# The per-layer gate of 704 tokens, computed as seven products per pair of output chunks

## The chip, the core and the metric

The kernel runs on one core of a Trainium2 chip. The core has a matmul engine (TensorE, PE in the profile), two engines for elementwise work (VectorE, DVE, and ScalarE, ACT), a slower one (GpSimd, POOL) and queues that start DMA transfers (here nearly all on SyncE, SP). The engines run side by side, each takes its own instructions in the order in which they stand in its queue, and semaphores tie them together. Matmuls write to PSUM, which has eight banks; everything else lies in SBUF. The metric is the device time of one execution in microseconds; the median of several runs counts.

## The reference

One layer of a decoder trunk is applied to 1056 tokens (1024 of a prompt, 32 of eight short continuations) with a width of 1024. What matters here is its last step, after mixing and feed-forward:

```
f = (silu(f @ w_gate) * (f @ w_up)) @ w_down
x = x + rms(f, n_ffn_post)
x = x + sigmoid(x @ w_ple_gate) * (p @ w_ple)
```

`x @ w_ple_gate` is the gate: a 1024 x 1024 product. `p @ w_ple` is the embedding product, from width 256 to 1024. The sum is the output `y`. Everything is float32; the kernel keeps that accuracy by splitting each operand into a high and a low part in a reduced format and adding three products (high x high, high x low, low x high).

## The kernel before

**Tiles.** Tokens lie along the free dimension, in three groups of 352: groups 0 and 1 (the 704 tokens of the title) and group 2. Channels lie on partitions, in 8 chunks of 128. One output tile is one chunk m of one group, 128 x 352. A full gate product for it takes 8 input chunks x 3 = 24 matmuls of 128 x 128 by 128 x 352; the embedding product takes 2 x 3 = 6.

**The stage.** Group 2 runs ahead of the others through the feed-forward part. At the end the order on TensorE is: the last down products of groups 0 and 1 (`last_down`), then `ple_out(0, m, 2)` for m = 1 to 7, then `ple_out(1, m, g)` for m = 7 down to 0 and g = 0, 1. `ple_out` (L1116) issues the embedding product (6 matmuls) and the gate product (24) into two PSUM banks; then ScalarE takes the sigmoid (L1126), VectorE multiplies (L1128) and adds x (L1130), and a DMA on SP writes the tile out (L1131).

**What comes ahead of it.** `ple_steps(g)` (L1062) is a generator, one for each group. It loads and splits the group's embedding input (`pl`, two DMAs, two casts, two subtractions), loads x from a scratch tensor, computes the norm, adds it to x for each half h of the channels (L1078, L1082: tiles `o` and `x2`), and splits the result with `f_operand` into operands (`fh`, `fl`) for TensorE, a cast on ScalarE (L164) and a subtraction on VectorE (L165), each 128 x 1408.

**The planner.** Between the products, `turn(n)` advances a clock counted in matmuls, and starts the next step of each pending generator (a chain) when it is due: each step names its load on VectorE, which is divided by a share (0.7 in this stage) and added up. `finish(...)` empties chains at once. So the planner sets where a step stands in the program. TensorE's order here is that of the program (`keep_in_program_order`); for the other engines the framework's scheduler takes the order of the program as a priority, and puts an instruction ahead of an earlier one when that one isn't ready by its reckoning.

**Weights.** A list ITEMS names the weights in the order of use. `need(k)` makes all items up to k + 4: a load of 512 KB into a raw buffer (tag `wr`, 3 buffers, `w_load`), then the split into high and low part (tag `wp`, 8 buffers of 4 KB per partition; `wh`, `wl`). A buffer comes free when its last reader is done. Activations lie in a pool of 27 buffers (tag `a`).

**Seven products.** The gate and up projections of the feed-forward part use a fast product for the tokens of groups 0 and 1 already: two output chunks (1, 2) and two token groups form a 2 x 2 block of products over the two channel halves, and seven half products replace eight. For it `t_sum` prepares four differences of operands (T1 to T4), and `w_sums` (L941) has GpSimd make four sums of weight halves in place in the raw buffers (L951, four operations of 128 x 512), which are then split like other weights (`sh`, `sl`). A quarter product is 4 x 3 = 12 matmuls (`ops4`). Before the change the per-layer gate does not use it.

Of the kernel before, what the change touches and what calls it, by code (L numbers as in the profile page):

```python
# [61 lines left out]
def trunk_kernel(  # L62
# [159 lines left out]
    for s, gs in WALK:  # L222
        pairs_of = []
        for i in range(SLAB):
# [9 lines left out]
            js = item("sums", jg, ju) if 0 in gs else None  # L234
# [16 lines left out]
    WPE[1] = [None] * 6 + WPE[0][6:]  # L251
    wp = WPE[0][-1][0]
    for m in reversed(range(6)):
        if m == 3:
            wp = direct_item(w_ple[0], [P, 2, 512])
        WPE[1][m] = wp, direct_item(w_pg[m], [P, KC, P])
# [3 lines left out]
    def need(k, ahead=LOOK):  # L260

        for i in range(len(made), min(k + ahead + 1, len(ITEMS))):
            kind, js = ITEMS[i]
            if kind == "direct":
                w_split(js[0])
                made[i] = pairs[js[0]]
            else:
                made[i] = w_sums(*(raws[ITEMS[j][1][0]] for j in js))
            for kind, js in ITEMS[i + 1 : i + 3]:
                if kind == "direct":  # L270
                    w_load(js[0])
        return made[k]
# [788 lines left out]

    def ple_steps(g):  # L1062

        pl = half(g, F32R, "pl")
        pls[g] = pl[:, 0:2, :], pl[:, 2:4, :]
        for k in range(2):
            pr = tmp(NS[g], "pr")
            nc.sync.dma_start(pr, p[:, k, OFF[g] : OFF[g + 1]])
            split(pl[:, k, :], pl[:, 2 + k, :], pr)
# [6 lines left out]
        for h in range(2):  # L1076
# [12 lines left out]
            x2s[g].append(f_operand(xh, g))  # L1089
            yield 10, 0  # L1090

# [24 lines left out]
    def ple_out(n, m, g):  # L1116
# [9 lines left out]
        se.activation(sg, pg[:, :N], AF.Sigmoid)  # L1126
# [5 lines left out]

    hid[:] = new_hid
    for m in range(FIRST):
        ple_out(0, m, 2)
# [6 lines left out]
    for m in range(FIRST, KC):  # L1142
        ple_out(0, m, 2)
# [93 lines left out]
```

## Time and profile before

| | |
|---|---|
| median of 3 runs | 1128.7 us (1128.33 to 1130.65) |
| profiled execution | 1130.04 us |
| its span | 1128.3 us |
| PE busy | 1116.1 us (99%) |
| DVE busy | 746.0 us (66%) |
| ACT busy | 440.4 us (39%) |
| POOL busy | 176.3 us (16%) |
| DMA, mean | 88 GB/s |

The span is the time from the first to the last recorded instruction; the execution's own time is a little longer. In rows of the profile, a line such as `L165 DVE TENSOR_TENSOR wl<-wr,wh` gives the line of the kernel, the engine, the operation and the tiles that it writes and reads, without their numbers. Times are in us from the start of the span; in square brackets stands how long the engine was idle before the instruction, and what ended that. L126 is the line of all matmuls, L164 and L165 are those of all splits, so tile names tell them apart: `wh` and `wl` are weights, `sh` and `sl` split sums, `fh` and `fl` operands, `o` the feed-forward output.

### The profile page before, as it was taken

What the parts mean: (1) busy time and instruction counts of PE and PEld (TensorE: products, weight loads), DVE (VectorE), ACT (ScalarE), POOL (GpSimd) and SP (SyncE); (2) the same over time, 40 slices, a digit from 0 to 9 for tenths busy, and PEclk for the clock granted to TensorE, in tenths of its full rate; (3) what the DMA queues carried; (4) which work ended last, traced back from release to release, by engine and by line L of the source; (5) the groups of instructions that cost most, each with busy time, mean ns of one, the idle gap of its engine ahead of it and who ended that gap; (6) DMA issues with size and microseconds to landing.
All of it is one profiled execution on the core that took longest, in us unless ns stands there. A gap on an engine that the chain in (4) does not pass through costs nothing.

```text
span 1128.3 us, 17581 instructions
## 1 busy us (share of the span) xinstructions
PE 1116.1 (99%) x7115; PEld 1093.3 (97%) x7115; DVE 746.0 (66%) x1238; ACT 440.4 (39%) x776; POOL 176.3 (16%) x149
## 2 busy tenths in 40 slices
PE   8999999999999999999999999999999999999998
PEld 8999987699999999999999999999999999999998
DVE  6667457876888965256555555557887877789532
ACT  7322266754555533331221313133424324366220
POOL 0045032200000032011111201111123123100000
PEclk9999999999999999999999999999999999999999
DMA  8121310172553312112110211112312222246211
GB/s 286 57 69 50 117 44 29 38 278 77 181 184 131 112 56 76 38 39 75 36 59 19 76 38 58 56 38 79 117 56 76 75 75 76 94 165 214 89 58 39
DMA packets 35265, 99.54 MB, mean 88 GB/s; under 512 B 4180, under 2 KB 14708, under 8 KB 35184
## 3 DMA queue, kind: packets, MB, share of 16 engines
q1 hardware_dynamic: 33856, 96.65, 25.3%
q10 hardware_dynamic: 1328, 1.77, 0.5%
q8 instruction: 56, 0.92, 0.3%
q14 instruction: 25, 0.20, 0.1%
HBM read 88.30 MB, written 10.11 MB: 87 GB/s over the span
## 4 chain that ended last, share of the span: by engine, by line
PE 91%; DVE 4%; ACT 2%; DMA 1%; issue 1%; POOL 1%; SPq 0%; POOLq 0%; ACTq 0%; DVEq 0%
PE b L126 90%; ACT a L625 1%; DMA xr<-in_x_dram 1%; DVE mx L617 1%; PE b L120 1%; POOL wr L951 0%; DVE a L662 0%; ACT wh L164 0%; DVE wl L165 0%; DVE h L364 0%; DMA c<-in_gains_dram 0%; DVE o L1078 0%; DVE x L1082 0%; POOL a L631 0%; DVE a L716 0%
## 5 line engine op out<-in xcount | busy, mean ns | idle before, releaser
L126 PE MATMUL b<-fh,wh 128*128 128x352 f32 x808 | 260.7, 323 | 0.0
L126 PE MATMUL b<-fh,wl 128*128 128x352 f32 x808 | 259.5, 321 | 0.0
L126 PE MATMUL b<-fl,wh 128*128 128x352 f32 x808 | 259.1, 321 | 0.0
L126 PE MATMUL b<-hid,wh 128*128 128x352 f32 x1056 | 253.0, 322 | 1.5 <-DVE o L1078 1.0
L164 ACT CAST wh<-wr 128x1024 fp32r<-128x1024 f32 (+1 forms) x139 | 142.9, 1030 | 262.7 <-PE b L126 226.8
L165 DVE TENSOR_TENSOR wl<-wr,wh 128x1024 fp32r<-128x1024 f32 (+1 forms) x139 | 170.7, 1231 | 61.9 <-ACT wh L164 61.7
L126 PEld LDWEIGHTS b<-hid,wh 128*128 128x128 f32 x1056 | 182.8, 188 | 2.4 <-PE b L126 1.3
L126 PE MATMUL b<-hid,wl 128*128 128x352 f32 x528 | 169.5, 321 | 0.0
L951 POOL TENSOR_TENSOR wr<-wr 128x512 f32<-128x512 f32 x44 | 63.5, 1442 | 628.1 <-DVE wl L165 452.5
L126 PEld LDWEIGHTS b<-fh,wl 128*128 128x128 f32 x808 | 152.0, 188 | 0.0
L126 PEld LDWEIGHTS b<-fl,wh 128*128 128x128 f32 x808 | 151.9, 188 | 0.0
L126 PEld LDWEIGHTS b<-fh,wh 128*128 128x128 f32 x808 | 151.6, 188 | 0.0
L1048 DVE TENSOR_TENSOR o<-o,b 128x352 f32<-128x352 f32 x240 | 115.0, 518 | 27.1 <-PE b L126 26.9
L126 PE MATMUL b<-fh,sh 128*128 128x352 f32 x352 | 113.6, 323 | 0.0
L126 PE MATMUL b<-fh,sl 128*128 128x352 f32 x352 | 113.2, 321 | 0.0
L126 PE MATMUL b<-fl,sh 128*128 128x352 f32 x352 | 112.9, 321 | 0.0
L126 PE MATMUL b<-h,wh 128*128 128x352 f32 x480 | 105.5, 326 | 1.0 <-ACT h L362 1.0
L165 DVE TENSOR_TENSOR sl<-wr,sh 128x1024 fp32r<-128x1024 f32 x44 | 53.8, 1223 | 75.4 <-ACT sh L164 75.4
L126 PEld LDWEIGHTS b<-hid,wl 128*128 128x128 f32 x528 | 99.3, 188 | 0.0
L164 ACT CAST sh<-wr 128x1024 fp32r<-128x1024 f32 x44 | 45.7, 1047 | 131.6 <-POOL wr L951 88.4
L126 PEld LDWEIGHTS b<-h,wh 128*128 128x128 f32 x480 | 82.5, 190 | 1.6 <-ACT h L362 1.3
L126 PEld LDWEIGHTS b<-fh,sl 128*128 128x128 f32 x352 | 66.3, 188 | 0.0
(152 smaller groups left out, 1597.8 us busy)
## 6 DMA issues: line engine op xcount, KB each, us to landing
wr<-in_w_gu_dram SPq DMA_DIRECT2D x64, 512.0 KB, 3.3
wr<-in_w_dn_dram SPq DMA_DIRECT2D x32, 512.0 KB, 3.3
wr<-in_w_pg_dram SPq DMA_DIRECT2D x14, 512.0 KB, 3.6
x<-in_x_dram SPq DMA_DIRECT2D x6, 704.0 KB, 10.9
x1d<-x SPq DMA_DIRECT2D x6, 704.0 KB, 3.6
x<-x1d SPq DMA_DIRECT2D x6, 704.0 KB, 6.4
out_y_dram<-yo SPq DMA_DIRECT2D x24, 176.0 KB, 1.9
wr<-in_w_out_b_dram SPq DMA_DIRECT2D x8, 512.0 KB, 3.9
```

Of the source, the lines that this page charges most:

```text
L120: ins = te.transpose(out, src, ident)
L126: ins = te.matmul(*args, **kw)
L164: fix(se.copy(hi, src))
L165: fix(ve.tensor_tensor(lo, src, hi.bitcast(F32), op=ALU.subtract))
L617: ve.tensor_reduce(mx, t, axis=AX.X, op=ALU.max)
L625: se.activation(t[:, c, :], t[:, c, :], AF.Exp, bias=nmx[:, c : c + 1], scale=scale, accum_out=sm[:, c : c + 1])
L951: ge.tensor_tensor(out, a, b, op=op)
L1048: ve.tensor_tensor(o, o, v, op=ALU.add)
```

## The change

For groups 0 and 1 the gate is computed as seven products per pair of chunks (1,0), (3,2), (5,4) and (7,6), as in the feed-forward part. Each pair has a first step (`ple_first`): two quarter products that give the tile of the odd chunk for group 0 directly, of which the first, P1, is kept. The first steps of all four pairs come ahead, for chunks 7, 5, 3 and 1. Then comes the rest of each pair (`ple_rest`), from (1,0) to (7,6): products with T4, T2, T3 and T1 and one with B22, and adds on VectorE, which give the other three tiles. In every tile the embedding product now stands behind the gate's (`ple_end`).

`ple_steps` no longer makes the operand B12, loads and splits the embedding input at its end, and for group 1 then makes T1, T2, T3 and T4 (`e_sum`), with each difference written over a tile of `o`. Of weights there are three new kinds: "home", the embedding weights, split into two buffers of the activation pool; "half", for which only the second half of the channels of the even chunk is split, into one buffer of `wp`; and "sums" on two raw weights. Only pair (1,0) finds its odd chunk's raw weight still there; the other pairs load it again. So the loads behind group 2's weights are: chunk 5, the embedding weights' first half, chunks 3, 1, 0, 3, 2, the embedding weights' second half, chunks 5, 4, 7, 6.

```diff
-    def w_split(j):
+    def w_split(j, home=None):
...
-        hi, lo = w_tile(shape, "wh"), w_tile(shape, "wl")
+        hi, lo = (home(shape, F32R) if home else w_tile(shape, s) for s in ("wh", "wl"))
...
+    PAIRS = ((1, 0), (3, 2), (5, 4), (7, 6))
+    W1 = {a: WPE[0][a] if a == KC - 1 else None for a, _ in PAIRS}
+    wp1 = WPE[0][-1][0]
+    wp0 = None
+    for a in (5, 3, 1):
+        if a == 3:
+            wp0 = item("home", add_plan(w_ple[0], [P, 2, 512]))
+        W1[a] = (wp0 if a < 4 else wp1), direct_item(w_pg[a], [P, KC, P])
+    W2 = {}
+    for a, b in PAIRS:
+        ja = ITEMS[W1[a][1]][1][0] if a == 1 else add_plan(w_pg[a], [P, KC, P])
+        jb = add_plan(w_pg[b], [P, KC, P])
+        if a == 5:
+            wp0 = item("home", add_plan(w_ple[1], [P, 2, 512]))
+        W2[a] = wp0, item("half", jb), item("sums", ja, jb)
...
-            if kind == "direct":
-                w_split(js[0])
+            if kind in ("direct", "home"):
+                w_split(js[0], act_tile if kind == "home" else None)
                 made[i] = pairs[js[0]]
+            elif kind == "half":
+                w_load(js[0])
+                t = w_tile([P, KC, P], "w2")
+                made[i] = t[:, 0:4, :], t[:, 4:8, :]
+                split(*made[i], raws[js[0]][:, 4:8, :])
             else:
-                made[i] = w_sums(*(raws[ITEMS[j][1][0]] for j in js))
+                for j in js:
+                    w_load(j)
+                made[i] = w_sums(*(raws[j] for j in js))
...
+    def e_sum(name):
+        (b11, b21), (b12, b22) = x2[0], x2[1]
+        (t1, t3), (t2, t4) = os_[0], os_[1]
+        out, a, b = {
+            "T1": (t1, b12, b11),
+            "T3": (t3, b22, b12),
+            "T2": (t2, b22, t1),
+            "T4": (t4, b21, t2),
+        }[name]
+        ve.tensor_tensor(out, a, b, op=ALU.subtract)
+        e7[name] = f_operand(out, 0)
...
     def ple_steps(g):
-        pl = half(g, F32R, "pl")
-        pls[g] = pl[:, 0:2, :], pl[:, 2:4, :]
-        for k in range(2):
-            pr = tmp(NS[g], "pr")
-            nc.sync.dma_start(pr, p[:, k, OFF[g] : OFF[g + 1]])
-            split(pl[:, k, :], pl[:, 2 + k, :], pr)
...
-            x2s[g].append(f_operand(xh, g))
+            if g == 2:
+                x2s[g].append(f_operand(xh, g))
+            elif (g, h) != (1, 0):
+                e7[f"B{h + 1}{g + 1}"] = f_operand(xh, g)
             yield 10, 0
+        pl = half(g, F32R, "pl")
...
+        yield 8, 0
+        if g == 1:
+            for name in ("T1", "T2", "T3", "T4"):
+                e_sum(name)
+                yield 20, 0
...
+    def ple_end(gate, wp, m, g):
         ph, pl = pls[g]
-        w = WPE[n][m]
-        wh, wl = need(w[0])
+        wh, wl = need(wp)
         cols = slice((m % 4) * P, (m % 4 + 1) * P)
-        pp, pg = bank(), bank()
+        pp = bank()
         gemm(pp[:, :N], ...)
-        gemm(pg[:, :N], ops8(need(w[1]), x2s[g]))
-        turn(30)
+        turn(6)
         sg = tmp(N, "sg")
-        se.activation(sg, pg[:, :N], AF.Sigmoid)
+        se.activation(sg, gate, AF.Sigmoid)
...
+    def ple_first(a):
+        wp, w = W1[a]
+        need(wp)
+        wg = need(w)
+        if not p1s:
+            p1s.append(half(0, s="p1"))
+        p1 = p1s[0][:, a // 2, :]
+        se.copy(p1, product(quarter(wg, 0), e7["B11"]))
+        c11 = tmp(N, "c11")
+        ve.tensor_tensor(c11, p1, product(quarter(wg, 1), e7["B21"]), op=ALU.add)
+        ple_end(c11, wp, a, 0)
+
+    def ple_rest(a, b):
+        wp, w, js = W2[a]
+        p1 = p1s[0][:, a // 2, :]
...
+        need(wp)
+        a22 = need(w)
+        p4 = product(a22, e7["T4"])
+        s = need(js)
+        add(p1, p1, product(s["S2"], e7["T2"]))
+        u3 = tmp(N, "u3")
+        add(u3, p1, product(s["S3"], e7["T3"]))
+        c21 = tmp(N, "c21")
+        add(c21, u3, p4)
+        ple_end(c21, wp, b, 0)
+        p5 = product(s["S1"], e7["T1"])
+        add(u3, u3, p5)
+        add(p1, p1, p5)
+        ple_end(u3, wp, b, 1)
+        add(p1, p1, product(s["S4"], e7["B22"]))
+        ple_end(p1, wp, a, 1)
...
     finish(chains[:1])
-    for m in reversed(range(KC)):
-        for g in (0, 1):
-            if g == 1 and m == KC - 1:
-                finish(list(chains))
-            ple_out(1, m, g)
+    for a in (7, 5, 3, 1):
+        ple_first(a)
+    finish(list(chains))
+    for a, b in PAIRS:
+        ple_rest(a, b)
```

More of the change, by code (lines that the diff above doesn't have):

```diff
@@ L1131, in ple_out, with product, add @@
         nc.sync.dma_start(y_o[:, m, OFF[g] : OFF[g + 1]], yo)
+    def ple_out(m, g):
+        wp, w = WPE[0][m]
+        need(wp)
+        pg = bank()
+        gemm(pg[:, :N], ops8(need(w), x2s[g]))
+        turn(24)
+        ple_end(pg[:, :N], wp, m, g)
+    def product(w, x):
+        ps = bank()
+        gemm(ps[:, :N], ops4(w, x))
+        turn(12)
+        return ps[:, :N]
+    p1s = []
+    def ple_first(a):
[12 more added lines that the diff above has]
+        p1 = p1s[0][:, a // 2, :]
+        def add(out, x, ps):
+            ve.tensor_tensor(out, x, ps, op=ALU.add)
+        need(wp)
+        a22 = need(w)
[13 more added lines that the diff above has]
+        ple_end(p1, wp, a, 1)
     hid[:] = new_hid
     for m in range(FIRST):
-        ple_out(0, m, 2)
+        ple_out(m, 2)
     for m in range(KC):
```

21 lines of the change are left out of this document (10 added, 11 removed).

## The prediction

> **What bounds the kernel now.** I read the page first (busy shares, slices), then the chain that ended last, then busy time by stretch for the stage that the change touches, then the order of single instructions on VectorE (DVE), ScalarE (ACT) and GpSimd (POOL) there.
>
> ```profile
> span 1128.3 us, 17581 instructions
> PE 1116.1 (99%) x7115; PEld 1093.3 (97%) x7115; DVE 746.0 (66%) x1238; ACT 440.4 (39%) x776; POOL 176.3 (16%) x149
> PEclk9999999999999999999999999999999999999999
> 1012.13 111.73 PE b L126 x701
> 1009.00:1047.10 38.10, 37.53 (x238) 36.99 (x237) 37.35 (x61) 21.59 (x32) 0.00 (x0) 1.00 0.62 215
> 1047.10:1066.30 19.20, 19.20 (x122) 19.20 (x121) 9.47 (x16) 4.34 (x7) 0.00 (x0) 1.00 0.26 85
> 1066.30:1123.90 57.60, 57.54 (x360) 57.25 (x358) 18.30 (x29) 10.25 (x18) 0.00 (x0) 1.00 0.16 57
> ```
>
> TensorE (PE) is busy for 99% of the span, and the last 111.73 us of the chain are PE alone (fourth row): a matmul fewer is time saved, as long as nothing else becomes late. The three rows of stretches give length, then PE, weight loads, DVE, ACT, POOL (each with its count), clock, DMA share and GB/s. They cut the end into the eight outputs of the last third of the tokens (to 1047.1) and the sixteen outputs that the change rewrites. DVE has no room in the first stretch (37.35 of 38.10 us), 9.7 us of room in the next 19.2 us, and much after that.
>
> ```profile
> 1047.08 0.47 ACT L1126 ACTIVATE sg<-b 128x352 f32<-128x352 f32 x1 [4.33 <-PE b L126]
> ...
> 1123.88 0.46 ACT L1126 ACTIVATE sg<-b 128x352 f32<-128x352 f32 x1 [4.34 <-PE b L126]
> 1123.88 0.47 ACT sg L1126
> ...
> 1124.38 0.53 DVE sg L1128
> ...
> 1124.93 0.52 DVE yo L1130
> ```
>
> Each sigmoid follows the last matmul of an output. Between the first and the last row lie 16 outputs of 30 matmuls: 76.80 / 16 = 4.80 us each, 0.160 us per matmul.
>
> **The saving.** The gate product of 704 tokens and 8 chunks is 16 x 24 = 384 matmuls before, 4 pairs x 7 x 12 = 336 after; the 96 of the embedding stay. 48 fewer x 0.160 = 7.7 us off PE. The end also shortens. Before, sigmoid, product and sum follow the last matmul: 1123.86 to 1125.45, 1.6 us. After, the last gate product is followed by an add (0.53) and the sigmoid (0.47) that run beside the six embedding matmuls (0.96), so about 1.15 us follow: 0.4 us less. Saving 8.1 us.
>
> **Work without a price of its own.** After the first stage there are 12 weight loads where there were 7; at a DMA share of 0.16 to 0.26 the bandwidth is there. The four copies on ACT, 28 adds on DVE and the smaller splits of the later pairs fall in a stretch where DVE used 18.30 of 57.60 us. The loads and splits of the embedding input move behind the operands: two DMAs, two casts and two subtractions per group, behind the x2 loads on SP's queue and before the T operands on DVE. Group 0's are due at the first embedding product, two gate products (3.8 us) later than before; I take nothing, and if that cover is gone PE waits for the 0.9 us of the two subtractions. DMAs of outputs wait in the same queue as weight loads; that is in the second rival.
>
> **What comes late: DVE ahead of the first pair.** PE reaches the second half of the new stage after four first steps of 30 matmuls, at 1047.1 + 19.2 = 1066.3, if it never waits. It then wants, in this order, the product with T4 and the half weight (1066.3), the products with sums S2 (1068.2) and S3. By then DVE has to do this:
>
> ```profile
> 1033.86 1.22 DVE L165 TENSOR_TENSOR wl<-wr,wh 128x1024 fp32r<-128x1024 f32 x1
> 1034.99 0.52 DVE L1128 TENSOR_TENSOR sg<-sg,b 128x352 f32<-128x352 f32 x1
> 1035.42 1.61 DVE L1078 TENSOR_TENSOR o<-o,b 128x1408 f32<-128x1408 f32 x1
> ...
> 1042.93 1.62 DVE L165 TENSOR_TENSOR fl<-x,fh 128x1408 fp32r<-128x1408 f32 x1
> 1044.46 0.52 DVE L1128 TENSOR_TENSOR sg<-sg,b 128x352 f32<-128x352 f32 x1
> ...
> 1051.24 1.63 DVE L165 TENSOR_TENSOR fl<-x,fh 128x1408 fp32r<-128x1408 f32 x1 [0.45 <-ACT fh L164]
> 1052.79 0.51 DVE L1128 TENSOR_TENSOR sg<-sg,b 128x352 f32<-128x352 f32 x1
> 1049.84 1.37 ACT L164 CAST fh<-x 128x1408 fp32r<-128x1408 f32 x1 [2.29 <-DVE x L1082]
> ```
>
> The distance from one start to the next is the price: 1.13 us for a weight split, 0.43 for a 352-wide operation, 1.53 for a 1408-wide one. The old work ends with group 1's last operand at 1052.8. One operand (B12) goes: -1.5. Three weight splits come in (the embedding weights that get their own place, chunks 3 and 1): + 3.4, so 1054.7. The T operands are four subtractions and four splits, 8 x 1.53 = 12.2: 1066.9. They are one after another with nothing to wait for but 1.37 us of ACT, which the next T covers except before the last.
>
> Can the weights overtake them? By the planner's counts (loads 6, 24, 10, 24, 10 over a share of 0.7, in matmuls) group 0's steps are all out when the first finish call of the new stage comes, so this call empties group 1's: all four T stand in the program ahead of the first steps, and the half weight and the sums stand behind them. On a DVE that is never out of ready work the half weight's split, 0.6 (half of 1.13), comes after T4: 1067.5. Only then may GpSimd overwrite the raw weights:
>
> ```profile
> 929.34 1.29 POOL L951 TENSOR_TENSOR wr<-wr 128x512 f32<-128x512 f32 x1 [13.92 <-DVE wl L165]
> 930.70 2.95 POOL L951 TENSOR_TENSOR wr<-wr,wr 128x512 f32<-128x512 f32 x2
> 933.73 1.46 POOL L951 TENSOR_TENSOR wr<-wr 128x512 f32<-128x512 f32 x1
> ...
> 936.30 1.22 DVE L165 TENSOR_TENSOR sl<-wr,sh 128x1024 fp32r<-128x1024 f32 x1 [1.84 <-ACT sh L164]
> 937.88 1.22 DVE L165 TENSOR_TENSOR sl<-wr,sh 128x1024 fp32r<-128x1024 f32 x1
> ```
>
> From the first sum to the end of the first split of sums: 937.52 - 929.34 = 8.2 us. So S2's weights are there at 1067.5 + 8.2 = 1075.7, where PE wants them at 1068.2: PE stands for 7.5 us in all, some 1.2 before T4's product and 6.3 before S2's. Everything else on PE is queued behind, since its order is fixed.
>
> This wait is nowhere in the trace of before, and a wait cannot be below nothing, so both ends: at the low end the half weight slips in at 1056 and only T4 is late, 1066.9 - 1066.3 = 0.6 us; at the high end the twelve evictions of the four first steps (12 x 0.43 = 5.2) go ahead of the half weight as well, 7.5 + 5.2 = 12.7 us. I take 7.5, which follows the program's order; in the 1.4 us before T4's split, where ACT is waited for, the half could win about 1 us.
>
> The rule against even the low end: a first sum took 4.58 us, not 1.29, when two 1408-wide splits of VectorE began just behind it:
>
> ```profile
> 397.11 4.58 POOL L951 TENSOR_TENSOR wr<-wr 128x512 f32<-128x512 f32 x1 [173.89 <-DMA wr<-in_w_gu_dram]
> 397.38 3.16 DVE L165 TENSOR_TENSOR fl<-y,fh 128x1408 fp32r<-128x1408 f32 x2
> ```
>
> The Trainium skill, page "GPSIMD Engine Reference", section "8. Key points", says that GpSimd shares its SBUF interfaces with VectorE and contends with VectorE instructions that have two SBUF inputs; these two rows agree. By that rule an early half weight would not help, because all eight T instructions have two SBUF inputs and would hold the sums to the same end, 7 us of wait; without it the low end stands at 0.6 us.
>
> **Later pairs.** A pair is 78 matmuls, 12.5 us. Its weights go round three raw buffers: sums and split 8.2 us, then the next load:
>
> ```profile
> 978.53 1.23 DVE L165 TENSOR_TENSOR sl<-wr,sh 128x1024 fp32r<-128x1024 f32 x1 [1.84 <-ACT sh L164]
> 979.78 0.33 SPq L174 DMA_DIRECT2D wr<-in_w_pg_dram  x1
> wr<-in_w_pg_dram SPq DMA_DIRECT2D x14, 512.0 KB, 3.6
> ```
>
> The load leaves 0.02 us after the split and lands in 3.6 (issue to landing): 11.8 us, less than 12.5. In the second pair the embedding weights' split (1.13) falls in: 12.9, so 0.4 us of wait once. Of a loop without waits nothing else is late.
>
> **Sum.** -7.7 - 0.4 + 7.5 + 0.4 = -0.2 us. The profiled execution took 1130.0 us (1.7 around its span), 1.3 over the median of 1128.7; it would come to 1129.8, and a median run to 1128.5. What a measurement can tell from no change is about 0.2%, 2.3 us, so this is no change.
>
> **Rivals.** (a) The cover holds. The half weight's buffer is free when chunk 5's first two products end, at about 1055.7. If the half split goes there and the sums run beside the T's, S2 is ready in time and only T4's 0.6 and the 0.4 remain: 1128.7 - 8.1 + 1.0 = 1121.6. For it: ACT and POOL are nearly idle then (4.34 and 0 of 19.2 us). Against it: the order of the program, and the 4.58 us row. Half-way, with the sums held by part of the T's, it is 1125.
>
> (b) Slower: the ring of three raw buffers. If each next load waits for the second split of sums (937.88 against 936.30, 1.6 us later), or as long behind an output's DMA on SP, and the half split (0.6) comes before the sums, the loop is 14.0 us. It decides from 12.5 on: 1.5 x 3 pairs = 4.5 us, 1128.5 + 4.5 - 0.4 = 1132.6. For it: DVE's backlog of evictions. Against it: the 0.02 us above.
>
> (c) The wait cools the PE:
>
> ```profile
> 5.89 3.04 PE L126 MATMUL b<-h,wh 128*128 128x352 f32 x8 [0.99 <-ACT h L362]
> ...
> 9.68 1.44 PE L126 MATMUL b<-h,wh 128*128 128x352 f32 x8
> ```
>
> Eight matmuls took 3.04 us at the kernel's start and 1.44 soon after, though the granted clock reads full there. After a wait of 6 us PE could start like that again: 1.6 us more, 1130.1. The Trainium skill, page "TensorE: Matmul & The Clock Gate", section "Why this matters for your kernels", warns of idle gaps over about 3 us between bursts, after which the clock is halved; no run here shows such a gap.
>
> That the products are not saved is excluded: the matmuls are counted out by the code.
>
> **How the numbers follow.** Forecast 0.35; (a) 0.20 and half-way 0.12; (b) 0.20; (c) 0.13. Faster by over 0.2%: (a), half-way and 0.03 of the forecast, 0.35. Slower: (b), 0.03 of the forecast and 0.05 of (c), 0.28. The rest, 0.37, is no change. The range runs from 1121.5, where half of (a) is left out, to 1132.6, where half of (b) is. The forecast's own range is 1127 to 1130.5 (the half in the gap, or a few evictions ahead).
>
> **What would show it.** 48 PE matmuls fewer. DVE without a gap from 1009 to about 1067, with four subtractions into o and four 1408-wide splits in a row. PE idle before the first product that reads the half weight, ended by DVE, and longer before the first product that reads a sum, ended by DVE's split of it; the first sum on POOL after 1063. Then PE without waits above 0.5 us, and about 1.2 us behind the last matmul. I am wrong if the first sum runs before 1060 (then a), if PE waits in each pair (then b), or if matmuls behind the wait take over 0.2 us each (then c).

## The result, and the profile after

After the change the median is 1134.96 us (1133.87 to 1135.93) where the kernel before, on the same chip, has 1128.66 (1128.33 to 1130.65): the ratio is 1.0054, with a 95% interval of 1.0041 to 1.0067. The forecast was 1128.5 with a range up to 1132.6. So the change costs about 6 us where no difference was forecast, and the time lies above the range.

The profiled execution took 1134.34 us, 0.6 under its median; that of before stood 1.3 over its own. The spans, 1132.5 and 1128.3, therefore show 4.2 us of the 6. The page of the kernel after, in the lines that answer to those of before:

```profile
span 1132.5 us, 17606 instructions
PE 1111.7 (98%) x7067; PEld 1087.4 (96%) x7067; DVE 783.6 (69%) x1283; ACT 454.3 (40%) x793; POOL 199.0 (18%) x165
PEclk9999999999999999999999999999999999999899
```

The 48 matmuls are gone (7115 to 7067). But PE is busy for 98%, not 99%, one slice of the clock row has an 8, and DVE has 37.6 us more to do. Busy time by stretch, cut where the new stage starts (1045.6), where PE stands, where it runs again, where its pace is normal again, and behind its last matmul (length; PE, weight loads, DVE, ACT, POOL, each with its count; clock, DMA share, GB/s):

```profile
1045.60:1061.30 15.70, 14.19 (x86) 13.29 (x84) 14.40 (x19) 8.65 (x11) 0.00 (x0) 1.00 0.29 96
1061.30:1067.30 6.00, 0.18 (x2) 0.00 (x0) 5.17 (x5) 1.72 (x3) 0.93 (x1) 0.87 0.00 0
1067.30:1072.50 5.20, 5.15 (x17) 5.15 (x18) 2.25 (x2) 0.71 (x2) 4.96 (x4) 0.50 0.00 0
1072.50:1126.90 54.40, 53.83 (x332) 52.97 (x331) 43.34 (x67) 18.32 (x28) 16.98 (x13) 1.00 0.32 105
```

PE stands still from 1061.3 to 1067.3, and for the 5.2 us behind that its granted clock is 0.50. PE's instructions in order of time (start, length; in brackets how long PE was idle, and what ended that):

```profile
1051.34 0.43 PE L126 MATMUL b<-pl,wh 128*128 128x352 f32 x1 [0.85 <-ACT pl L164]
1052.30 0.43 PE L126 MATMUL b<-pl,wh 128*128 128x352 f32 x1 [0.53 <-DVE pl L165]
...
1067.35 2.13 PE L126 MATMUL b<-pl,a 128*128 128x352 f32 x6 [5.87 <-ACT p L1196]
1069.28 0.49 PE L126 MATMUL b<-fh,wh 128*128 128x352 f32 x1
1069.57 0.49 PE L126 MATMUL b<-fl,wh 128*128 128x352 f32 x1
...
1075.81 0.43 PE L126 MATMUL b<-fh,w 128*128 128x352 f32 x1
...
1077.84 0.32 PE L126 MATMUL b<-fh,sh 128*128 128x352 f32 x1
...
1114.09 0.40 PE L126 MATMUL b<-fh,w 128*128 128x352 f32 x1 [0.49 <-DVE p L1206]
...
1125.77 1.12 PE L126 MATMUL b<-pl,a 128*128 128x352 f32 x6
```

Four things are to be seen. The first embedding product waits for its input (`pl`), first for the cast and then for the subtraction. The long wait stands before the embedding product of chunk 3 and is ended by ScalarE's copy of a first product (L1196, the tile `p1`). Behind it the matmuls start 0.29 us apart, and from 1072.5 on 0.16 again. And the first product that reads a sum (`sh`, 1077.84) does not wait at all; T4's product before it (1075.81) stood for some 0.2 us.

Why a copy on ScalarE ends the long wait stands in the other engines' order:

```profile
1043.20 0.42 SPq L1124 DMA_DIRECT2D pr<-in_p_dram  x1
1048.80 0.49 ACT L164 CAST pl<-pr 128x352 fp32r<-128x352 f32 x1 [6.58 <-DMA pr<-in_p_dram]
...
1065.58 1.36 ACT L164 CAST fh<-o 128x1408 fp32r<-128x1408 f32 x1 [4.85 <-DVE o L1091]
1066.85 1.16 ACT L1196 COPY p<-b 128x352 f32<-128x352 f32 x3
...
1063.93 1.62 DVE L1091 TENSOR_TENSOR o<-x,o 128x1408 f32<-128x1408 f32 x1
...
1066.98 2.14 DVE L165 TENSOR_TENSOR fl<-o,fh 128x1408 fp32r<-128x1408 f32 x1 [0.83 <-ACT fh L164]
1069.04 0.51 DVE L1198 TENSOR_TENSOR c<-p,b 128x352 f32<-128x352 f32 x1
1066.37 1.27 POOL L968 TENSOR_TENSOR wr<-wr 128x512 f32<-128x512 f32 x1 [89.83 <-DVE w L165]
1074.10 1.23 DVE L165 TENSOR_TENSOR sl<-wr,sh 128x1024 fp32r<-128x1024 f32 x1 [4.55 <-ACT sh L164]
1075.24 0.51 DVE L1167 TENSOR_TENSOR sg<-sg,b 128x352 f32<-128x352 f32 x1
```

A first step fills three PSUM banks: P1, the second product, the embedding product. Chunks 7 and 5 fill six, chunk 3's first two products the other two. None comes free until ScalarE has copied P1 and VectorE has added to it, and both engines first finish the T operands: ScalarE waits 4.85 us for the difference T4, casts it and then copies three P1 in a row; VectorE's first add (L1198) is at 1069.04, behind T4's split. So the ninth product, chunk 3's embedding, has no bank. It runs at the first copy.

The same happens once more. T4's product needs the bank of chunk 7's embedding product, which comes free with VectorE's multiply at 1075.24. That multiply stands behind the split of the first sum, for which VectorE waited 4.55 us, with evictions behind it. By these rows PE stands there for only 0.2 us because it comes late itself.

The end, too, is longer. From PE's last matmul (1125.77 + 1.12 = 1126.89) to the end of the last sum (1129.56) there are 2.7 us; before there were 1.6. The chain that ended last goes, from 1114 us on, back and forth between DVE and ACT and no longer through PE:

```profile
1127.35 0.52 DVE p L1206
...
1127.94 0.51 ACT sg L1165
...
1129.03 0.53 DVE yo L1169
```

The account on PE: the stage has 432 matmuls, 69.1 us at 0.160, and took 81.0 from 1045.6 to its last start (1126.57). The difference is 2.2 us around the first embedding product (1049.5 to 1052.3), 6.0 before chunk 3's, 2.4 of slow matmuls (18 of them, 0.293 - 0.160 each), 0.65 before the last pair, and some 0.6 in small parts, the 0.2 before T4's product among them. These are the places where PE's time went, not prices that could be taken off one by one: a part that goes can come back in the next wait. So: -7.7 + 11.9 + 1.1 at the end = +5.3 us; in the profiled execution the stage began 1.5 us earlier than in that of before, which leaves 3.8 of the spans' 4.2.

### The profile page after: what moved, and what is told of

The parts are those of the page before. It is cut to its first block, busy times and chain, and to the rows that moved or that the text cites. A ratio compares the mean times of both kernels' runs of the same rounds, so it can differ in the third digit from the quotient of the medians.

```text
span 1132.5 us, 17606 instructions
## 1 busy us (share of the span) xinstructions
PE 1111.7 (98%) x7067; PEld 1087.4 (96%) x7067; DVE 783.6 (69%) x1283; ACT 454.3 (40%) x793; POOL 199.0 (18%) x165
## 5 line engine op out<-in xcount | busy, mean ns | idle before, releaser
L126 PE MATMUL b<-fh,wh 128*128 128x352 f32 x712 | 230.5, 324 | 0.0
L126 PE MATMUL b<-fl,wh 128*128 128x352 f32 x712 | 228.8, 321 | 0.0
L126 PE MATMUL b<-fh,wl 128*128 128x352 f32 x712 | 228.7, 321 | 0.0
L126 PEld LDWEIGHTS b<-fl,wh 128*128 128x128 f32 x712 | 134.4, 189 | 0.0
L126 PE MATMUL b<-fh,sh 128*128 128x352 f32 x416 | 134.3, 323 | 0.0
L126 PEld LDWEIGHTS b<-fh,wh 128*128 128x128 f32 x712 | 134.2, 188 | 0.0
L126 PEld LDWEIGHTS b<-fh,wl 128*128 128x128 f32 x712 | 134.1, 188 | 0.0
L126 PE MATMUL b<-fh,sl 128*128 128x352 f32 x416 | 133.5, 321 | 0.0
L126 PE MATMUL b<-fl,sh 128*128 128x352 f32 x416 | 133.3, 320 | 0.0
L126 PEld LDWEIGHTS b<-fl,sh 128*128 128x128 f32 x416 | 78.3, 188 | 0.0
```

What stands on the lines that cost most here:

```text
L126: ins = te.matmul(*args, **kw)
```

## The experiments

Three theories. **Q**: the T operands stand in ScalarE's and VectorE's queues ahead of the copies and adds that free the banks; another order would cure it. **W**: the weights of the sums are late whatever VectorE does, and when one wait goes, PE stands at the first product with a sum (the prediction, too, had them late, but because of the T operands). **D**: VectorE and ScalarE simply have more to do in this stretch than PE's work covers, in whatever order.

### No T operands

```diff
-            for name in ("T1", "T2", "T3", "T4"):
-                e_sum(name)
-                yield 20, 0
+            for name, b in (("T1", "B11"), ("T2", "B21"), ("T3", "B22"), ("T4", "B11")):
+                e7[name] = e7[b]
```

> Leaves out the four differences T1 to T4 and their splits (the products that want them read operands that exist already), so the output of groups 0 and 1 is wrong; all matmuls, weights and sums stay. Theory Q (the T operands stand ahead in the queues of ACT and DVE, and the copies that free PSUM banks wait behind them): the 6.0 us wait in front of chunk 3's embedding product and the 2.3 us at half clock behind it go, 1134.9 - 8.3 = 1126.6, and somewhat less as DVE lags less at the end. Theory W (the weights of the sums are late whatever DVE does): GpSimd's sums still start at 1065 or later, PE waits some 5 us before S2's product, 1131 to 1133.

Measured: 1126.12 us (1124.94 to 1126.68), ratio to before 0.9965 [0.9953, 0.9976]. PE's waits and GpSimd's first sum:

```profile
1050.20 0.43 PE L126 MATMUL b<-pl,wh 128*128 128x352 f32 x1 [0.85 <-ACT pl L164]
1051.92 0.66 PE L126 MATMUL b<-pl,wh 128*128 128x352 f32 x1 [1.29 <-DVE pl L165]
1059.19 1.29 POOL L968 TENSOR_TENSOR wr<-wr 128x512 f32<-128x512 f32 x1 [83.41 <-DVE w L165]
```

Only the two waits for the embedding input are left. Without the eight T operations the half weight is split by 1059, the sums follow at their normal pace, and no product waits for one. W falls: the weights are late only because VectorE makes the T operands, as the prediction had it. The time is near Q's 1126.6, but this run takes away the order and the work together, so it doesn't separate Q from D. These operands cost 1.0054 - 0.9965, about 0.9% or 10 us, more than the 7.7 us that the seven products save.

### The clock behind the wait

Twenty-four matmuls whose result is overwritten are added in front of chunk 3's second product.

```diff
-    def product(w, x):
+    def product(w, x, idle=0):
...
+        for _ in range(idle):
+            mm(ps[:, :N], w[0][:, 0, :], x[0][:, 0, :], start=True, stop=True)
...
-        ve.tensor_tensor(c11, p1, product(quarter(wg, 1), e7["B21"]), op=ALU.add)
+        ve.tensor_tensor(c11, p1, product(quarter(wg, 1), e7["B21"], 24 if a == 3 else 0), op=ALU.add)
```

> Puts 24 matmuls whose result is overwritten ahead of the second product of chunk 3, where PE stands 6.0 us afterwards for a PSUM bank: 3.8 us of the wait are filled, 2.2 us stay. If the slow matmuls behind the wait (0.293 us each at a granted clock of 0.50) come from the wait, they run at 0.160 us now: 18 x 0.133 = 2.4 us less, 1132.5. If the clock has another cause, the time is 1134.9 or a little more.

Measured: 1133.8 us (1132.44 to 1134.87), ratio 1.0035 [1.0023, 1.0047], where the changed kernel has 1.0054 [1.0041, 1.0067].

```profile
1067.43 1.56 PE L126 MATMUL b<-pl,a 128*128 128x352 f32 x6 [2.04 <-ACT p L1198]
1068.79 0.50 PE L126 MATMUL b<-fh,wh 128*128 128x352 f32 x1
...
1075.89 0.43 PE L126 MATMUL b<-fh,w 128*128 128x352 f32 x1 [0.89 <-ACT p L1198]
```

The embedding product starts at the same time (1067.43 against 1067.35), so the wait ends when it did. But the added matmuls didn't keep the clock up. A wait of 2.0 us is left, and behind it the matmuls run slowly again, only for less time: the embedding product takes 1.56 us, not 2.13, and from 1068.79 on ten more start 0.293 us apart. PE loses some 0.8 us less by that, and gives it back in a wait of 0.9 us for the next bank: T4's product starts at 1075.89, where in the changed kernel it starts at 1075.81. So this run doesn't separate the clock from the wait. What it shows is that running faster here brings PE no further: by these rows the slow matmuls have no price of their own, since they fill time in which PE would wait for that bank. The 2 us between the two ratios, whose intervals touch, are in no row up to there, and where they come from stays open.

### The embedding input back at the head

The loads and splits of `pl` stand at the head of `ple_steps` again, as before the change; the rest is the changed kernel.

> Moves the loads and splits of the embedding input back to the head of each group's steps. If the 1.9 us that PE waits for them in chunk 7's first step is a price of its own: 1133.0. Theory Q: the next wait ends when ACT is through with T4's cast, so PE comes 1.9 us earlier and waits longer; DVE's four 0.43 us splits ahead of the T operands are gone as well, so T4 comes up to 1.7 us earlier: 1133.2 to 1134.9.

Measured: 1133.62 us (1132.89 to 1134.15), ratio 1.0034 [1.0021, 1.0047].

```profile
1065.52 2.13 PE L126 MATMUL b<-pl,a 128*128 128x352 f32 x6 [5.86 <-ACT p L1195]
```

There is no wait ahead of this row any more. The wait for a bank is as long as it was and the clock behind it as slow (2.13 again); it only comes 1.8 us earlier. It does so because T4's cast comes earlier by as much (1063.75 for 1065.58): VectorE no longer has to wait for the embedding input, nor to split it between the T operands. If only PE's own first wait had gone, the bank would have come free no sooner. So the moved input costs 2 us, by way of the T operands as much as of PE.

### The T operands spread by the planner

The call that empties the chains in front of the first steps goes, so that the planner places the T operands between the first steps.

```diff
-    finish(chains[:1])
     for a in (7, 5, 3, 1):
```

> Leaves out the finish call in front of the first steps, so that the planner hands out group 1's last operand and the T operands one by one between the products. The order of ACT and DVE then has the copies, evictions, the half weight and the sums of pair (1,0) ahead of T2 to T4. Theory Q: the bank wait of 6.0 us goes; a wait for T4 of some 2 us takes its place, clock full: 1128 to 1129. Theory D (DVE has more work than time before the first pair, in whatever order): T4 comes 5 us later than now because the evictions go first, PE waits 5 to 7 us before T4's product and runs at half clock after it: 1133 to 1136.

Measured: 1143.17 us (1142.6 to 1144.8), ratio 1.0121 [1.0106, 1.0136], the slowest of all and above the range of either theory.

```profile
1083.66 0.66 PE L126 MATMUL b<-fh,w 128*128 128x352 f32 x1 [16.08 <-ACT fh L164]
1086.06 0.66 PE L126 MATMUL b<-fl,w 128*128 128x352 f32 x1 [1.73 <-DVE fl L165]
...
1061.94 4.09 POOL L968 TENSOR_TENSOR wr<-wr,wr 128x512 f32<-128x512 f32 x2
1062.17 2.71 DVE L1091 TENSOR_TENSOR o<-x,o 128x1408 f32<-128x1408 f32 x1
```

The wait for a bank is gone, as Q says, but PE then waits 16.1 us for the cast and 1.7 for the split of T4: the kind of wait that D says, and some three times the size. Evictions, weight splits and sums have gone ahead of it on VectorE. Besides, GpSimd's sums now run beside the T operations and both take longer: two sums 4.09 us where they take 2.83 in the kernel without T operands, a difference 2.71 where alone it takes 1.62. The Trainium skill, page "GPSIMD Engine Reference", section "8. Key points", has GpSimd contend with VectorE instructions that read two SBUF inputs; these rows agree.

### Two first steps ahead, two behind

```diff
-    for a in (7, 5, 3, 1):
+    while "B22" not in e7:
+        next(chains[0][0])
+    for a in (7, 5):
+        ple_first(a)
+    finish(list(chains))
+    for a in (3, 1):
         ple_first(a)
```

> The changed kernel, with the first steps of chunks 7 and 5 put into the queues ahead of the T operands, those of 3 and 1 behind them. Theory Q: the copies and adds of two chunks no longer stand behind the T operands, so their banks are freed in time, the wait of 6.0 us falls under 2 us, and the time is 4 us or more below the changed kernel's (ratio to before 1.002 or less). Theory D: the T operands end later by what was put ahead of them (3 to 5 us), and PE waits instead before the product of the fourth T operand or for a bank of chunk 3: 5 us or more in all, with the clock of the stretch at 0.6 or lower; ratio 1.004 to 1.010.

Measured: 1132.62 us (1131.23 to 1133.74), ratio 1.0028 [1.0019, 1.0037].

```profile
1072.08 0.66 PE L126 MATMUL b<-fh,w 128*128 128x352 f32 x1 [5.01 <-ACT fh L164]
1073.76 0.66 PE L126 MATMUL b<-fl,w 128*128 128x352 f32 x1 [1.01 <-DVE fl L165]
```

The wait for a bank is gone, and 5.0 + 1.0 us of wait for T4's cast and split have come in its place: this is what D says of the place and the size, and Q, by which less than 2 us should be left, fails. The ratio is between the two, under D's 1.004 and over Q's 1.002. I had not allowed for the end: here it is 4.9 us from PE's last matmul start (1124.49) to the end of the span, where the changed kernel has 5.9, and PE doesn't wait before the last pair.

### T's subtractions on GpSimd

```diff
-        ve.tensor_tensor(out, a, b, op=ALU.subtract)
+        ge.tensor_tensor(out, a, b, op=ALU.subtract)
         e7[name] = f_operand(out, 0)
```

> The changed kernel with the four subtractions of the T operands on GpSimd, which is idle until 1066 us, instead of VectorE. VectorE loses 4 x 1.62 = 6.5 us of work there; on GpSimd, at 1.29 us for 512 elements, one of 1408 takes about 3.5 us, the four 14 us, so the last would end at about 1063.5 as now, if the two engines didn't hold each other up. Theory D (VectorE's amount of work): the wait of 6.0 us falls to 3 us or less, ratio 1.001 to 1.004. Theory Q (ScalarE's copies stand behind the cast of the fourth T operand in its queue, whoever makes it): the wait stays at 5 us or more, as that cast comes no earlier, ratio 1.005 to 1.009. If the two engines hold each other up as in the run with the operands spread (GpSimd's 1.29 becoming 2.6 to 4.1), the fourth operand comes later still: ratio 1.007 to 1.012.

Measured: 1137.64 us (1136.56 to 1138.71), ratio 1.0078 [1.0064, 1.0091].

```profile
1054.39 3.46 POOL L1091 TENSOR_TENSOR o<-x,x 128x1408 f32<-128x1408 f32 x1
1055.28 2.96 DVE L1169 TENSOR_TENSOR yo<-sg,x 128x352 f32<-128x352 f32 x1
...
1058.16 4.57 DVE L165 TENSOR_TENSOR fl<-x,fh 128x1408 fp32r<-128x1408 f32 x1
1063.21 0.66 PE L126 MATMUL b<-pl,wh 128*128 128x352 f32 x1 [7.10 <-DVE pl L165]
```

It is the third case: the two engines hold each other up. A sum of 352 that takes 0.52 us alone takes 2.96, a split of 1408 takes 4.57 where it takes 1.62, and with the split of the embedding input just ahead (1052.36, 2.45 us where it takes 0.52) these three lose 7.3 us, more than the 6.5 us taken off VectorE. PE waits 7.1 us, now for the embedding input whose subtraction stands behind that split. This run therefore doesn't separate Q from D; it shows that GpSimd's idle time here is no free place.

### More cover: the pair (7, 6) computed directly

The pair (7, 6) gets four full gate products again, at the head of the stage and with the embedding input at its old place; the other three pairs keep the seven products, and the T operands are spread.

```diff
-    PAIRS = ((1, 0), (3, 2), (5, 4), (7, 6))
+    PAIRS = ((1, 0), (3, 2), (5, 4))
...
-    finish(chains[:1])
-    for a in (7, 5, 3, 1):
+    for g in (0, 1):
+        if g:
+            while len(x2s[1]) < 2:
+                next(chains[0][0])
+        for m in (7, 6):
+            ple_out(m, g)
+    for a in (5, 3, 1):
         ple_first(a)
```

> The pair of chunks 7 and 6 is computed directly again (four gate products of 24 matmuls, with the embedding's behind them, at the head of the stage); the other three pairs take seven products, first steps in the order 5, 3, 1; the embedding input is loaded at the head of its steps again; the T operands are spread between the outputs instead of standing in one block. 36 matmuls are saved instead of 48 (5.8 us), and 14.4 us more of PE work stand between the sub-vectors and the first product that reads a T operand. Theory D (VectorE and ScalarE have more to do before that product than PE's cover holds, in whatever order): with 14.4 us more cover the waits of 6.0 us and the cold stretch behind them go, and the time is 5.8 us below before less 0 to 2.5 us at the end and in the pairs: ratio 0.995 to 0.998. Theory Q (only the order in the queues of ScalarE and VectorE matters, a block of T operands ahead of the copies): the T operands still stand ahead of evictions of the first steps, PE waits 3 to 6 us for a bank there, ratio 1.000 to 1.003.

Measured: 1125.78 us (1125.56 to 1126.39), ratio 0.9968 [0.9956, 0.9981]; on another chip, beside the next kernel:

> The kernel with the pair (7, 6) computed directly once more, beside the next on the same chip: ratio 0.9968, within 0.0012.

1126.26 us (1125.62 to 1127.11), ratio 0.9978 [0.9970, 0.9987], near the upper end of what was expected. The stretches where the changed kernel stands and then runs at half clock, in this one (columns as above):

```profile
1060.00:1067.00 7.00, 7.00 (x46) 7.00 (x44) 6.68 (x8) 4.09 (x5) 0.00 (x0) 1.00 0.34 122
1067.00:1075.00 8.00, 8.00 (x51) 8.00 (x51) 7.42 (x10) 3.20 (x5) 1.83 (x2) 1.00 0.08 26
```

PE is busy throughout at full clock, and VectorE still has 14.1 of 15 us to do: it needed the cover. This is what D says. The run alone doesn't refute Q, since the order has changed here too: the first copy of a P1 runs at 1068.00, ahead of T4's cast at 1069.33. It also has the embedding input at its old place, which was worth 2 us above. What refutes Q are the two runs that change the order alone (spread, and two ahead): there the wait only moved, from the bank to T4. Order and cover together remove it. This kernel beats both the kernel before and the changed one, with 36 matmuls saved instead of 48. Of the 5.8 us that this is worth it keeps 2.5 to 3.6.

### The end

Where do the rest of these 5.8 us go? The kernel with (7, 6) direct has 6.0 us from PE's last matmul start (1118.61) to the end of the span (1124.6); before, there were 4.8 (1123.52). VectorE waits 2.3 us at the start of the last pair, for the cast of its first sum, with evictions behind it:

```profile
1104.49 1.23 DVE L165 TENSOR_TENSOR sl<-wr,sh 128x1024 fp32r<-128x1024 f32 x1 [2.27 <-ACT sh L164]
```

Five runs bear on that. First the embedding product behind the gate's, alone, in the kernel before:

```diff
-        pp, pg = bank(), bank()
-        gemm(pp[:, :N], [(wh[:, k, cols], wl[:, k, cols], ph[:, k, :], pl[:, k, :]) for k in range(2)])
+        pg = bank()
         gemm(pg[:, :N], ops8(need(w[1]), x2s[g]))
-        turn(30)
+        turn(24)
+        pp = bank()
+        gemm(pp[:, :N], [(wh[:, k, cols], wl[:, k, cols], ph[:, k, :], pl[:, k, :]) for k in range(2)])
+        turn(6)
```

> The kernel before with one part of the change alone: in each of the 24 last outputs the embedding product is issued behind the gate's 24 matmuls, not ahead of them. The number of matmuls and the loads stay. By the step on the end: the sigmoid runs beside the last six matmuls, so 0.3 to 0.5 us less stand behind the last one and nothing else moves: ratio 0.999 to 1.000. If the order of the two products itself costs (a bank that comes free later, the embedding input read elsewhere): PE shows waits in front of outputs, ratio over 1.001.

Measured: 1129.26 us (1129.0 to 1130.25), ratio 1.0003 [0.9994, 1.0012]. The end in the trace:

```profile
1123.14 0.32 PE L126 MATMUL b<-pl,wl 128*128 128x352 f32 x1
1123.57 0.52 DVE L1130 TENSOR_TENSOR sg<-sg,b 128x352 f32<-128x352 f32 x1 [3.72 <-PE b L126]
1124.12 0.52 DVE L1132 TENSOR_TENSOR yo<-sg,x 128x352 f32<-128x352 f32 x1
```

From PE's end (1123.46) to the end of the sum (1124.64) there are 1.2 us instead of 1.6. The mechanism is there; its 0.4 us are below what the times can tell. So the order of the two products isn't what lengthens the end of the changed kernel.

Next, the changed kernel without GpSimd's additions:

> The changed kernel without GpSimd's additions for the sums of the per-layer gate's weights in the first 704 tokens (the sums hold what lay in their memory; the splits behind them stay). Theory D: the T operands are late by VectorE's own work; the wait of 6.0 us for a bank and the cold stretch stay, as the additions begin only at their end; VectorE's waits of about 2.3 us for the splits of later pairs go, and with them 0.5 to 1.5 us of the later pairs and the end: ratio 1.003 to 1.005. If GpSimd's additions slow VectorE enough to matter: the wait is under 4 us and the ratio 1.002 or less.

Measured: 1132.2 us (1131.47 to 1133.18), ratio 1.0024 [1.0013, 1.0035], below D's 1.003 to 1.005, with this at the old place:

```profile
1068.29 2.13 PE L126 MATMUL b<-pl,a 128*128 128x352 f32 x6 [6.81 <-ACT p L1198]
```

The wait for a bank is there, 0.9 us longer since splits of sums now stand ahead of the copies. What goes is at the end: 4.6 us from PE's last start (1126.29) to the end of the span, not 5.9, and no wait before the last pair. So the additions cost the end 1.3 us here; the splits behind them are still made in this kernel. They need not cost it: the run with two first steps behind makes all additions and has an end of 4.9.

Then three tries to have the sums of the last pair earlier, made from the kernel with (7, 6) direct. In the first, the splits for the next pair are issued behind the current pair's outputs.

```diff
         ple_end(c21, wp, b, 0)
+        if a < 5:
+            need(W2[a + 2][1], 0)
...
         ple_end(p1, wp, a, 1)
+        if a < 5:
+            need(W2[a + 2][2], 0)
```

> The same kernel, with the splits of the next pair's sums and half weight issued behind the current pair's outputs instead of ahead of its first product, their loads as early as before. Claim: the end is 1.5 us longer than before (6.0 against 4.4 us from PE's last group to the end of the span) because VectorE stood 2.27 us before the split of the last pair's sums (1102.2 to 1104.5) with that pair's evictions behind it and never caught up. If so, the end falls to 5 us or less, PE's wait of 0.6 us before the last pair goes, and the time is 1 to 2 us below the kernel it is made from (ratio to before 0.995 to 0.996). Rival: the end is long by its own number of alternating steps on VectorE and ScalarE; then the end stays at 6 us and the time within 0.7 us.

1125.72 us (1125.25 to 1125.91), ratio 0.9972 [0.9962, 0.9983], end 6.0 us: the same as the kernel that it is made from. The scheduler put the split ahead of the pair's evictions all the same (VectorE now waits 3.6 us for it), so the change did not do what it was for. In the second, made from the same kernel, the last pair's raw weights get tiles outside the ring of three buffers.

```diff
-        t = wpool.tile(shape, F32, tag="wr", bufs=W_RAW, name=nm("wr"))
+        t = act_tile(shape) if j in roomy else wpool.tile(shape, F32, tag="wr", bufs=W_RAW, name=nm("wr"))
...
         W2[a] = wp0, item("half", jb), item("sums", ja, jb)
+        if a == 5:
+            roomy.update((ja, jb))
```

> The kernel with the pair (7, 6) computed directly, with the two raw weights of its last pair (5, 4) loaded into free tiles of the activations' pool instead of the ring of three raw buffers. There, the two loads were issued at 1091.4 and 1092.8 us, when buffers came free, GpSimd's additions followed at 1097.7 and VectorE's split of the sums at 1104.5, with the pair's evictions behind it. Claim: the ring of raw buffers makes the last pair late; with the loads earlier, GpSimd's last additions start before 1094 us, VectorE's wait of 2.3 us goes, PE's wait of 0.6 us before the last pair goes, the end from PE's last group to the end of the span falls from 6.0 to 5 us or less, and the time is 1 to 2 us below: ratio to before 0.9955 to 0.9965 where the kernel it is made from had 0.9968 and 0.9978. Rival: the end is long by its own alternating steps on VectorE and ScalarE: end 5.7 us or more, time within 0.7 us.

1126.67 us (1125.64 to 1128.47), ratio 0.9980 [0.9971, 0.9989], end 6.0 us.

```profile
1097.93 1.30 POOL L970 TENSOR_TENSOR a<-a 128x512 f32<-128x512 f32 x1 [8.60 <-DVE w L165]
```

The loads leave at 1070.4 and 1087.2 instead of 1091.4 and just behind it, but GpSimd begins no earlier, because VectorE's split of the half weight (`w`, 1097.16) ends its wait. The ring of buffers is not the cause. Both times the rival named beforehand, an end that is long by its own steps going back and forth between VectorE and ScalarE, still fits. In the third, made from the second, that one split goes ahead of the sums of pair (3, 2).

```diff
+    H = {a: item("half", J2[a][1]) for a in (1, 5)}
+    S = {1: item("sums", *J2[1])}
+    H[3] = item("half", J2[3][1])
+    S[3] = item("sums", *J2[3])
+    S[5] = item("sums", *J2[5])
```

> The kernel of the run before (pair (7, 6) direct, the last pair's raw weights in tiles of their own), with the half weight of the last pair (5, 4) split ahead of the sums of the pair (3, 2), not behind them. In the run before, that pair's second load was issued at 1087.2 us, but GpSimd's additions began at 1097.9, when VectorE had split the half weight (1097.2), which stood in VectorE's queue behind the other pair's splits. Claim: this queue makes the last pair's sums late, and their split holds up the evictions behind it. If so, GpSimd's last additions start before 1093 us, VectorE's wait of 2.3 us and PE's of 0.5 us go, the end falls from 6.0 to 5 us or less, and the ratio to before is 0.9955 to 0.997 where the run before had 0.9980 [0.9971, 0.9989]. Rival: the end is long by its own alternating steps on VectorE and ScalarE: end 5.7 us or more, ratio 0.9975 to 0.9985.

1128.35 us (1126.28 to 1129.21), ratio 0.9993 [0.9984, 1.0002].

```profile
1083.62 2.15 POOL L975 TENSOR_TENSOR a<-a 128x512 f32<-128x512 f32 x1
1086.39 1.29 POOL L975 TENSOR_TENSOR wr<-wr 128x512 f32<-128x512 f32 x1 [0.62 <-DVE w L165]
...
1095.95 0.63 PE L126 MATMUL b<-fh,w 128*128 128x352 f32 x1 [2.64 <-DVE p L1211]
...
1121.93 0.52 DVE L1211 TENSOR_TENSOR p<-p,b 128x352 f32<-128x352 f32 x1 [0.73 <-PE b L126]
```

The claim holds for the end, and that rival falls: with the last sums done at 1085.8, VectorE waits for PE at the end (last row), and PE's last start (1122.53) is 4.5 us before the end of the span. But the ratio misses what I expected: on GpSimd the last pair's sums went ahead of pair (3, 2)'s, which then came late, with 2.6 us of wait and a slow stretch behind it. So, as far as these runs show, the long end is the queue of sums and splits on GpSimd, ScalarE and VectorE. An order of it that costs nothing at either place was not found.

## Why the prediction was wrong, by its own steps

**What bounds the kernel.** Right: PE alone set the time before, and without the T operands the time falls.

**The saving.** The 48 matmuls are gone, and undisturbed ones still start 0.160 us apart. The 0.4 us at the end are there when that part is made alone (1.2 us for 1.6, with the embedding behind). In the changed kernel the step fails: 2.7 us follow the last matmul, because VectorE reaches the end with a backlog. The term was -0.4 and measured +1.1.

**Work without a price of its own.** This step failed. I took nothing for the moved embedding input and named 0.9 us if its cover were gone; it cost 2.2 us in the trace and 2 us when moved back. I counted the cover on PE (two products, 3.8 us), but not when the load leaves and lands: it left SP's queue at 1043.2, just behind a weight load, took 5.6 us, and ScalarE's cast, which waited 6.6 us for it, began at 1048.8, when PE was about to use it. Nor did I count that VectorE, waiting for that cast, starts the T operands later. The copies and adds failed too, in another way. I priced them by VectorE's free time later on and did not ask what holds their PSUM banks until they run.

**What comes late.** This is the step that failed most: the place was wrong, and that the size is near is luck, since the two waits are made of different terms. I had PE standing 7.5 us, 1.2 before T4's product and 6.3 before the first sum; it stood 6.0, for a bank before chunk 3's embedding product, and behind that for neither. VectorE's load was counted nearly: T4's split ended at 1069.1 for 1066.9 (the half weight slipped in ahead of it, as allowed for, and its last split took 2.14 us beside GpSimd), and the first split of sums at 1075.3 for 1075.7. Counted from the start of the stage, which came 1.5 us earlier in this execution, these are 3.7 and 1.1 us late. What was missing is that the block of T operands stands ahead of the copies as well. I saw that order for the half weight and not for the evictions, though the same paragraph says that the T operands come ahead of the first steps in the program; a count of the eight banks against three products per step would have shown it. The consequence is a wrong path, not only a wrong place. By the forecast PE does T4's product at 1067.5, inside the time in which the sums are made, and S2's at 1075.7. In the trace the banks hold back the first steps and T4's product as well, until VectorE's multiply behind the first split of sums, and S2's product follows T4's at 1077.84. From the start of the stage that is 32.2 us where I had 28.6: 3.6 of the 5.5 us by which the sum below is off.

**Later pairs.** 0.4 us once, measured 0.65 once. But the cause is VectorE's queue, not the embedding weights' split.

**The rivals.** (a) did not come: the half weight was split at 1065.5, behind the differences of all four T operands. In the run with two first steps ahead it was split at 1057.7 and the sums ran beside the T operands, but then T4 was late. (b), the ring of three raw buffers, was not it: GpSimd waited 5.45 us for a load once, and loads made earlier for the last pair (in the kernel with (7, 6) direct) changed nothing. It gave the nearest time, 1132.6, but for a wrong reason. (c) came true beside the forecast, not instead of it: 2.4 us of slow running for the 1.6 that I took from the kernel's start. I gave it a chance of its own when it followed from the forecast. But as a price to add it is not shown: in the run with the added matmuls PE ran slowly for less time and began T4's product no earlier. The Trainium skill's rule in "TensorE: Matmul & The Clock Gate", "Why this matters for your kernels", was the one to give weight: by it the forecast's own 6 us wait brings a half clock. The trace agrees with it for this wait.

**The sum.** With the measured terms: -7.7 + 1.1 (end) + 2.2 (input) + 6.0 (bank) + 2.4 (clock) + 0.65 (last pair) + 0.6 = +5.3 us where I had -0.2. As places on PE, the three terms put at nothing or in a rival (input, clock, end) outweigh the whole error, and the bank in place of the forecast wait takes 1.5 off. As a path, 3.6 us of it arise before S2's product, by the banks and the later T operands, and 1.5 at the end.

## What to carry to other kernels

Before evictions are called hidden, count the PSUM banks that the products fill until the first eviction can run, and look at what stands ahead of it in its engine's queue. In these runs waits of PE of 2.0, 2.6, 5.0, 6.0 and 16.1 us each brought a stretch of matmuls 0.29 us apart with them. A forecast that has such a wait has to have that stretch too, and then ask whether something behind it would have made PE wait anyway. A transform that saves matmuls at one place and needs operands made on other engines has to be set against the work that covers these operands: here three pairs with 14 us more of PE's work as cover gain 0.2 to 0.3%, and four pairs at once lose 0.5%.

## What the runs showed of the hardware

The clock halves after shorter waits than I had thought. After 6.0 us the granted clock was 0.50 for 5.2 us and matmuls started 0.293 us apart. After the 2.0 us in the run with added matmuls ten of them, from 1068.79 on, started as far apart. After the 2.6 us in the last run above it was 0.50 for 3.1 us:

```profile
1093.30:1095.90 2.60, 0.01 (x1) 0.00 (x0) 1.66 (x3) 0.82 (x1) 0.00 (x0) 1.00 0.00 0
1095.90:1099.00 3.10, 3.05 (x10) 3.08 (x11) 2.45 (x6) 1.86 (x4) 0.00 (x0) 0.50 0.00 0
```

The Trainium skill's section named above puts the bound at about 3 us of gap; here shorter ones were enough, and the measurement decides.

GpSimd and VectorE slow each other by two to nearly six times: with T's subtractions on GpSimd, 0.52 us became 2.96 and 1.62 became 4.57 on VectorE; with the T operands spread, a first sum of 1.29 us became 2.56 on GpSimd.
